# One PSUM rotation of four banks for the attention's scores and for the work beside it

## The chip, the cores and the metric

The kernel runs on one core of a Trainium2 chip. The metric is the device time of one launch in microseconds (us); the median of several runs is compared.

## The reference, cut to what matters

Two layers of a streaming encoder run over 1024 prompt frames and 64 sample frames (T = 1088 columns here). Each layer projects the normalised input once, feeds three token mixers, merges them and adds the result back:

```
h = rmsnorm(x, norm_in)
hq, hkv, g_a, u_b, g_b, qkv_c, g_c, g_mix = split_cols(h @ w_in)
o_a = mla_attend(...) * silu(g_a)          # 8 heads, whole past
o_b = pool_mix(u_b, ...) * silu(g_b)       # trailing means, one linear map a group
o_c = ca_attend(...) * silu(g_c)           # 4 heads, band of chunks, bias
gates = sigmoid(g_mix)
m = gates[0] * (o_a @ w_o_mla) + gates[1] * (o_b @ w_o_pool) + gates[2] * (o_c @ w_o_ca)
x = x + m @ w_out
x = x + sigmoid(rmsnorm(x, ple_norm) @ w_ple_gate) * (ple @ w_ple_proj)
```

## The kernel before, in words

Activations lie feature by token, 128 features to a tile. In each layer a long projection (`gemm`, L404) comes first, then the attention with other work beside it, then the merge of the latent heads' output (`merge`), then the output projection and the `ple` block (again `gemm`). Most products are sums of three matmuls of split operands (`mm3`, L132 to L134).

`attention` runs 108 units a layer, one unit for each head and block of 128 queries: 36 of the four chunk heads, then 72 of the eight latent heads. A unit's `scores` takes one or two tiles `S` of the pool `pg` (L1034 for chunk heads, L1105 for latent ones); DVE takes their minimum (L1036, L1109); ACT makes the exponentials (L857); DVE the reciprocal of the sum (L864) and POOL the product with it (L865). Two units later TensorE transposes the result into `pT` (L891), which ACT and DVE split into `PT`, and multiplies it with the values (`pv`, L925, L917).

Three further pieces of work go beside this. `ple_proj` makes `pps` (32 tiles of 6 matmuls, copied by ACT at L1444 into one of two buffers `o` and stored as `pp`). `pool_branch` makes `pbm` (6 tiles), from which `mbo` is stored. `merge_bc` loads `mbo` and the chunk heads' output through two buffers `of`, splits them into eight tiles `oh`, `ol`, and then does 16 works: a work loads two gates `g` (tags `g8` and `g16`, two buffers each, 272 KB a load), makes four tiles `mps` of 6 matmuls, multiplies them into the gates on DVE (L1424), adds the gates on POOL (L1426) and stores the sum as `mb` from the buffer `g8`. A gate buffer is free for the work after next only when the store from it has landed. `merge` loads `mb` after the attention.

The order on each engine is not written out: the scheduler of the tile framework hoists or delays instructions by priority, and pools hand out their buffers in the order of the program text. In the program text `beside` (which is all of `pps`, `pbm` and `mps`) is called by `attention` ahead of the scores of the 14th unit from the end (`BESIDE = 14`). Only the first steps of the two generators run earlier, through `advance`. DMAs all go through SP's queue in one order; a DMA that waits holds those behind it.

PSUM has eight banks. In the attention, before the change, `pg` has three for `S`, `pn` two for `pT`, `po` one for `pps`, `pbm` and `mps`, and `pv` two.

Of the kernel before, what the change touches and what calls it, by code (L numbers as in the profile page):

```python
# [10 lines left out]
F32 = mybir.dt.float32  # L11
# [35 lines left out]
AT_E = (("K00", KT, 1), ("Q00", T, 1), ("Q10", T, 1), ("K10", KT, 1))  # L47

BANKS = {"gemm": (("pg", 3), ("pn", 2)), "keys": (("pg", 2), ("pn", 2), ("po", 2)),
         "attn": (("pg", 3), ("pn", 2), ("po", 1), ("pv", 2))}  # L50
LATE = 100
NEAR, BESIDE = 8, 14
PVE = ("v",)
# [22 lines left out]
class K:  # L76
# [1223 lines left out]
    def pool_branch(self, l, sp):  # L1300
        nc, d = self.nc, self.d
        zd = self.z_d[l]
        W = 1120
        for j in range(2):
            wr = sp.tile([128, 128], F32, tag="pw", name="pw")
            self.ld(wr, d["poolw"][l, j])
            u = sp.tile([128, W], F32, tag="pu", name="pu")
            nc.gpsimd.memset(u[:, 0:16], 0.0)
            nc.gpsimd.memset(u[:, 1040:1041], 0.0)
            self.ld(u[:, 16:1040], zd[Z_UB + j][:, :1024])  # L1310
            self.ld(u[:, 1041:1056], d["hist"][l, j])
            self.ld(u[:, 1056:], zd[Z_UB + j][:, 1024:])
            self.st(d["poolp"][l, j], u[:, 1025:1040])
            self.st(d["pools"][l, j], u[:, 1105:1120])
            g = self.r
            self.ld(g, zd[Z_GB + j])
            yield
            a = sp.tile([128, W], F32, tag="pa", name="pa")
            b = sp.tile([128, W], F32, tag="pb", name="pb")

            def dbl(dst, src, s, p0=0):
                n = 2
                for i in range(n):
                    c0, c1 = max(s, W // n * i), W // n * (i + 1)
                    nc.gpsimd.tensor_add(dst[p0:, c0:c1], src[p0:, c0:c1], src[p0:, c0 - s:c1 - s])
                nc.scalar.copy(dst[p0:, :s], src[p0:, :s])

            dbl(a, u, 1)
            yield
            if j == 0:  # L1330
                dbl(b, a, 2, 64)
                nc.scalar.copy(b[:64], a[:64])
            else:
                dbl(b, a, 2)
                yield
                dbl(a, b, 4)
                yield
                dbl(b, a, 8, 64)
                nc.scalar.copy(b[:64], a[:64])
            yield  # L1340
            pl = sp.tile([128, T], F32, tag="pl", name="pl")
            sc = self.pinv[:, j, 16:17]
            nc.vector.scalar_tensor_tensor(pl[:, :1024], b[:, 16:1040], sc, u[:, 16:1040], op0=ALU.mult, op1=ALU.subtract)
            nc.vector.scalar_tensor_tensor(pl[:, 1024:], b[:, 1056:], sc, u[:, 1056:], op0=ALU.mult, op1=ALU.subtract)
            nc.vector.tensor_mul(b[:, 16:32], b[:, 16:32], self.pinv[:, j, :16])
            nc.vector.tensor_sub(pl[:, :16], b[:, 16:32], u[:, 16:32])
            yield
            hi = sp.tile([128, T], F32R, tag="pa", name="ph")
            lo = sp.tile([128, T], F32R, tag="pb", name="plo")
            n = 2  # L1350
            for i in range(n):
                c = slice(T // n * i, T // n * (i + 1))
                self.split(pl[:, c], hi[:, c], lo[:, c], "a", 'v')
            wh = sp.tile([128, 2, 128], F32R, tag="pwh", name="pwh")
            self.split(wr, wh[:, 0], wh[:, 1])
            yield
            yield
            o = sp.tile([128, T], F32, tag="pl", name="po")
            for c0, c1 in CH3:
                ps = self.po.tile([128, 512], F32, tag="o", name="pbm")  # L1360
                self.mm3(ps[:, :c1 - c0], wh[:, 0], wh[:, 1], hi[:, c0:c1], lo[:, c0:c1])
                nc.vector.scalar_tensor_tensor(o[:, c0:c1], ps[:, :c1 - c0], self.gn[l][:, G_PS + j:G_PS + j + 1],
                                               g[:, c0:c1], op0=ALU.mult, op1=ALU.mult)
                yield
            self.ld(self.mbo_d[l][j], o)
# [37 lines left out]
    def merge_bc(self, l, sp):  # L1403
        nc, d = self.nc, self.d
        zd = self.z_d[l]

        def weights(m):
            return self.weights(d["wbc"][l, m], 4)

        def gates(m, ti):  # L1410
            gs = []
            for k in (8, 16):
                gs.append(sp.tile([128, H], F32, tag=f"g{k}", name="g"))
                self.ld(gs[-1], zd[Z_MIX + k + m][:, ti * H:ti * H + H])
            return gs

        def work(ti, m, hl, w, gs):
            for g, b in zip(gs, (0, 2)):
                for c in range(2):
                    cc = slice(c * C, c * C + C)  # L1420
                    ps = self.po.tile([128, 512], F32, tag="o", name="mps")
                    for k in (b, b + 1):
                        self.mm3(ps[:, :C], w[:, 0, k], w[:, 1, k], hl[k][0][:, cc], hl[k][1][:, cc], k == b, k == b + 1)
                    nc.vector.tensor_mul(g[:, cc], g[:, cc], ps[:, :C])  # L1424
                yield
            nc.gpsimd.tensor_add(gs[0], gs[0], gs[1])  # L1426
            self.ld(self.mb_d[l][m][:, ti * H:ti * H + H], gs[0])

        yield from self.ahead(sp, [self.mbo_d[l][0], self.mbo_d[l][1], self.o_d[l][0], self.o_d[l][1]], weights, work, gates)

    def ple_proj(self, l, sp, op):
        nc, d = self.nc, self.d

        def weights(m):
            return self.weights(d["wpp"][l, m], 2)

        def work(ti, m, hl, w, _):
            o = op.tile([128, H], F32, tag="po", name="o", bufs=2)
            for c in range(2):
                cc = slice(c * C, c * C + C)  # L1440
                ps = self.po.tile([128, 512], F32, tag="o", name="pps")
                for k in range(2):
                    self.mm3(ps[:, :C], w[:, 0, k], w[:, 1, k], hl[k][0][:, cc], hl[k][1][:, cc], k == 0, k == 1)
                nc.scalar.copy(o[:, cc], ps[:, :C])  # L1444
            yield
            self.ld(self.pp_d[l][m][:, ti * H:ti * H + H], o)

        yield from self.ahead(sp, [d["p"][l, 0], d["p"][l, 1]], weights, work, els=("g", "v"))
# [234 lines left out]
```

## Time and profile before

| what | us |
|---|---|
| median of 3 runs | 2279.34 (2278.78 to 2288.59) |
| the profiled execution: time | 2290.6 |
| the profiled execution: span of the core | 2288.8 |
| PE busy in the span | 2163.4 (95%) |
| PE weight loads busy | 2083.9 (91%) |
| DVE busy | 1743.5 (76%) |
| ACT busy | 1176.3 (51%) |
| POOL busy | 693.4 (30%) |

PE is TensorE's matmuls. The span begins with the first instruction and ends with the last. The attention takes two stretches of it, one for each layer. A table of stretches gives the length, then the busy time of each engine with its count of instructions, then the granted clock of TensorE as a share of 2.4 GHz, the DMA engines' busy share, and GB/s.

### The profile page before, as it was taken

The numbers are of one execution on the slowest core, as the hardware profiler recorded it, in microseconds if no ns is written. First come the engines' busy times: TensorE is split into PE (matmuls) and PEld (weight loads), VectorE is DVE, ScalarE is ACT, GpSimd is POOL, SyncE is SP. The second block draws the span as 40 slices with busy tenths as digits, with TensorE's granted clock in tenths as the row PEclk, the third lists the DMA queues.
The fourth block names the chain that finished last, engine by engine and source line by source line (L and its number), as shares of the span: only waits on it lengthen the run. The fifth ranks groups of instructions, "written<-read, shape, count | busy, mean of one in ns | idle before, by whom it ended". The sixth has DMA issues, their size and how long they took to land.

```text
span 2288.8 us, 44876 instructions
## 1 busy us (share of the span) xinstructions
PE 2163.4 (95%) x16326; PEld 2083.9 (91%) x16326; DVE 1743.5 (76%) x3590; ACT 1176.3 (51%) x2491; POOL 693.4 (30%) x918
## 2 busy tenths in 40 slices
PE   5999999999789999899989999999988899999998
PEld 4999999999588998899979999999987889998998
DVE  8777888676568889887686678876747788889764
ACT  6234455454667666335453343555546776653341
POOL 0000044676455554000000000547574665430000
PEclk8999999999899999999989999999999999999999
DMA  3534546455966764545634345554569666645472
GB/s 125 185 110 135 185 142 193 129 158 143 279 196 183 198 172 136 204 173 179 210 107 139 118 158 173 165 157 127 159 179 276 199 186 179 186 162 186 144 232 74
DMA packets 222191, 385.81 MB, mean 169 GB/s; under 512 B 30404, under 2 KB 114196, under 8 KB 221972
## 3 DMA queue, kind: packets, MB, share of 16 engines
q1 hardware_dynamic: 221972, 382.95, 54.2%
q8 instruction: 130, 2.13, 0.4%
q14 instruction: 89, 0.73, 0.1%
HBM read 248.16 MB, written 134.70 MB: 167 GB/s over the span
## 4 chain that ended last, share of the span: by engine, by line
PE 62%; DMA 15%; DVE 13%; ACT 4%; issue 3%; POOL 2%; SPq 1%; DVEq 0%; ACTq 0%; POOLq 0%
PE g L404 36%; PE g L372 6%; PE S L1105 3%; PE pv L925 3%; PE pT L891 3%; DMA pp<-o 3%; DMA g<-z 2%; PE mps L132 1%; DMA mb<-g 1%; SPq L87 1%; DVE wop L121 1%; DMA r<-rd 1%; PE mps L134 1%; PE mps L133 1%; PE vps L1074 1%
## 5 line engine op out<-in xcount | busy, mean ns | idle before, releaser
L110 ACT CAST wop<-wraw 128x512 fp32r<-128x512 f32 (+1 forms) x238 | 143.8, 606 | 259.3 <-PE g L404 154.8
L865 POOL TENSOR_SCALAR P<-P,st 128x640 f32<-128x640 f32 (+8 forms) x216 | 155.3, 723 | 203.0 <-DVE st L864 122.3
L121 POOL TENSOR_TENSOR wop<-wraw,wop 128x512 fp32r<-128x512 f32 (+1 forms) x80 | 99.3, 1244 | 382.9 <-ACT wop L110 382.4
L121 DVE TENSOR_TENSOR PT<-pT,PT 128x512 fp32r<-128x512 f32 (+4 forms) x360 | 167.6, 473 | 39.3 <-ACT PT L110 37.3
L121 DVE TENSOR_TENSOR wop<-S,wop 128x512 fp32r<-128x512 f32 x178 | 141.6, 795 | 68.1 <-ACT wop L110 67.6
L110 ACT CAST wop<-S 128x512 fp32r<-128x512 f32 x202 | 124.6, 618 | 123.4 <-PE g L404 119.6
L110 ACT CAST PT<-pT 128x512 fp32r<-128x512 f32 (+4 forms) x360 | 147.0, 420 | 54.4 <-PE pT L891 47.8
L404 PE MATMUL g<-B11h,wop 128*128 128x272 f32 x832 | 152.4, 294 | 16.5 <-ACT B11h L112 12.7
L925 PE MATMUL pv<-PT,V 128*128 128x256 f32 x928 | 165.4, 297 | 2.5 <-DVE PT L121 1.6
L1105 PE MATMUL S<-K,Q 96*128 96x384 f32 (+5 forms) x672 | 158.8, 353 | 6.5 <-ACT P L857 6.5
L132 PE MATMUL mps<-oh,wop 128*128 128x272 f32 x512 | 155.2, 304 | 8.6 <-DVE g L1424 3.9
L891 PE MATMUL pT<-ident,P 128*128 128x128 f32 x936 | 158.5, 279 | 2.9 <-DVE PT L121 1.2
L404 PE MATMUL g<-T3h,wop 128*128 128x272 f32 x832 | 153.9, 293 | 7.7 <-ACT T3h L110 5.0
L404 PE MATMUL g<-B21h,wop 128*128 128x272 f32 x832 | 156.3, 298 | 4.8 <-ACT P L416 4.6
L404 PE MATMUL g<-T1h,wop 128*128 128x272 f32 x832 | 151.7, 293 | 3.6 <-DVE z L681 1.9
L404 PE MATMUL g<-T2h,wop 128*128 128x272 f32 x832 | 152.9, 294 | 2.1 <-ACT T2h L110 1.8
L404 PE MATMUL g<-B22h,wop 128*128 128x272 f32 x832 | 151.0, 293 | 0.0
L404 PE MATMUL g<-T4h,wop 128*128 128x272 f32 x832 | 149.7, 291 | 0.0
L134 PE MATMUL mps<-oh,wop 128*128 128x272 f32 x512 | 148.3, 290 | 0.0
L857 ACT ACTIVATE P<-S,st 128x384 f32<-128x384 f32 (+5 forms) x224 | 126.7, 572 | 38.2 <-DVE st L853 27.1
L925 PEld LDWEIGHTS pv<-PT,V 128*128 128x128 f32 x928 | 131.1, 191 | 11.0 <-DVE PT L121 6.2
L404 PEld LDWEIGHTS g<-B11h,wop 128*128 128x128 f32 x832 | 124.0, 192 | 18.1 <-ACT B11h L112 13.2
(291 smaller groups left out, 6591.0 us busy)
## 6 DMA issues: line engine op xcount, KB each, us to landing
wraw<-win SPq DMA_DIRECT2D x88, 512.0 KB
z<-z SPq DMA_DIRECT2D x96, 272.0 KB
g<-z SPq DMA_DIRECT2D x64, 272.0 KB
z<-z SPq DMA_DIRECT2D x24, 544.0 KB
Q<-q SPq DMA_DIRECT2D x32, 408.0 KB
K<-k SPq DMA_DIRECT2D x32, 400.0 KB
k<-hl SPq DMA_DIRECT2D x48, 256.0 KB
q<-hl SPq DMA_DIRECT2D x64, 192.0 KB
```

What stands on the lines that cost most here:

```text
L87: self.nc.sync.dma_start(out=self.raw(out), in_=self.raw(in_))
L110: nc.scalar.copy(out, src)
L121: e.tensor_sub(out, src, hi)
L132: mm(ps, lhsT=wh, rhs=xh, start=first, stop=False)
L134: mm(ps, lhsT=wl, rhs=xh, start=False, stop=last)
L372: self.nc.tensor.matmul(ps[:, c, :C], lhsT=hl[kh][:, w, kb, :], rhs=b[:, kb, c * C:(c + 1) * C], start=kh + k == 0, stop=kh == 1 and k == 11)
L404: nc.tensor.matmul(ps[:, c, :C], lhsT=hl[:, w, kb, :], rhs=b[:, kb, c * C:(c + 1) * C], start=k == 0 and not more, stop=k == 11, skip_grou ...
L857: nc.scalar.activation(u.p[:, c * w:c * w + w], x, AF.Exp, bias=st[:, 0:1], scale=-1.0, accum_out=st[:, 2 + c:3 + c])
L865: nc.gpsimd.tensor_scalar(u.p[:, :n], u.p[:, :n], st[:, 4:5], 1.0, op0=ALU.mult, op1=ALU.mult)
L891: nc.tensor.transpose(ps[:, j], p[:, c0:c0 + 128], self.ident)
L925: nc.tensor.matmul(ps[:, :w], lhsT=v(b), rhs=grp[b // 4][:, b % 4, j, :w], start=i + j == 0, stop=i == len(bl) - 1 and j == 1)
L1105: nc.tensor.matmul(ps[:, :ww], lhsT=q[0:96, q0:q0 + 128], rhs=k[0:96, k0 + c * w:k0 + c * w + ww], start=i == 0, stop=i == 2 and not diag)
```

## The change

The pool `po` goes, its bank is given to `pg`, and `pps`, `pbm` and `mps` are taken from `pg` under the tag `s` of the scores. No instruction is added or removed.

```
 BANKS = {"gemm": (("pg", 3), ("pn", 2)), "keys": (("pg", 2), ("pn", 2), ("po", 2)),
-         "attn": (("pg", 3), ("pn", 2), ("po", 1), ("pv", 2))}
+         "attn": (("pg", 4), ("pn", 2), ("pv", 2))}
...
             for c0, c1 in CH3:
-                ps = self.po.tile([128, 512], F32, tag="o", name="pbm")
+                ps = self.pg.tile([128, 512], F32, tag="s", name="pbm")
...
                     cc = slice(c * C, c * C + C)
-                    ps = self.po.tile([128, 512], F32, tag="o", name="mps")
+                    ps = self.pg.tile([128, 512], F32, tag="s", name="mps")
...
                 cc = slice(c * C, c * C + C)
-                ps = self.po.tile([128, 512], F32, tag="o", name="pps")
+                ps = self.pg.tile([128, 512], F32, tag="s", name="pps")
```

The change moves instructions. On PE, inside the third latent head of the first layer, this stood before (`S` are scores, `mps` the merge's matmuls):

```order
L925 MATMUL pv<-PT,V 128x256
L891 MATMUL pT<-ident,P 128x128 x4
L1105 MATMUL S<-K_8383,Q_8381 128x384
L1105 MATMUL S<-K_8384,Q_8381 128x384
L1105 MATMUL S<-K_8383,Q_8382 128x384
L925 MATMUL pv<-PT,V 128x256 x7
L891 MATMUL pT<-ident,P 128x128 x4
L925 MATMUL pv<-PT,V 128x256
L132 MATMUL mps<-oh,wop 128x272
L133 MATMUL mps<-ol,wop 128x272
L134 MATMUL mps<-oh,wop 128x272
```

and this stands there now:

```order
L925 MATMUL pv<-PT,V 128x256
L1105 MATMUL S<-K_8380,Q_8378 128x384
L1105 MATMUL S<-K_8381,Q_8378 128x384
L1105 MATMUL S<-K_8380,Q_8379 128x384
L925 MATMUL pv<-PT,V 128x256 x7
L891 MATMUL pT<-ident,P 128x128 x7
L1105 MATMUL S<-K_8380,Q_8378 128x384
L1105 MATMUL S<-K_8381,Q_8378 128x384
L1105 MATMUL S<-K_8380,Q_8379 128x384
```

No `pps`, `pbm` or `mps` is left among the first 94 units of a layer. All of them stand behind the scores of the 94th unit: first `pps` with the transposes and values of the last units in flight, then the rest of `pps`, `pbm`, and 384 `mps` matmuls in one block. On PE, the end of that block and the scores of the 95th unit behind it (before, `mps` stood between such scores):

```order
L134 MATMUL mps<-oh,wop 128x272
L132 MATMUL mps<-oh,wop 128x272
L133 MATMUL mps<-ol,wop 128x272
L134 MATMUL mps<-oh,wop 128x272
L1105 MATMUL S<-K_9706,Q_9704 128x288
L1105 MATMUL S<-K_9707,Q_9704 128x288
L1105 MATMUL S<-K_9706,Q_9705 128x288
```

On SP, in the same layer, the stores of `mb` and the loads of gates stood before between the loads of the next head (`Q`, `K`):

```order
L87 DMA mb_109<-g 128x544
L87 DMA g<-z_105 128x544 x2
L90 DMA o_111<-o 128x1088
L87 DMA acc<-z_105 128x1088
L87 DMA wraw<-woa 128x4x128
L87 DMA mb_109<-g 128x544
L87 DMA g<-z_105 128x544 x2
L87 DMA Q_9707<-q_117 96x1088
L87 DMA Q_9708<-q_117 96x1088
```

and now they follow each other, with the loads of all heads ahead of them:

```order
L87 DMA mb_109<-g 128x544
L87 DMA g<-z_105 128x544 x2
L87 DMA wraw<-woa 128x4x128
L87 DMA mb_109<-g 128x544
L87 DMA g<-z_105 128x544 x2
L87 DMA mb_109<-g 128x544
```

What moved is the place of the beside work: it was spread over the attention, and is now one block ahead of the last 14 units.

## Rows read from the trace of the kernel before

**Rows 1.** Table of stretches: chunk and latent part of layer 0, then of layer 1.

```profile
core 0: us, PE busy (x) PEld busy (x) DVE busy (x) ACT busy (x) POOL busy (x), PEclk, DMA share, GB/s
590.90:692.60 101.70, 85.65 (x577) 76.78 (x577) 71.70 (x262) 68.53 (x201) 50.12 (x82) 0.95 0.84 228
692.60:910.00 217.40, 210.55 (x1584) 193.09 (x1583) 184.18 (x529) 146.06 (x427) 115.59 (x164) 1.00 0.60 171
...
1724.60:1823.00 98.40, 84.44 (x578) 75.71 (x578) 71.81 (x262) 68.53 (x201) 50.36 (x82) 0.97 0.86 236
1823.00:2040.00 217.00, 210.96 (x1584) 193.07 (x1583) 184.82 (x529) 146.54 (x427) 115.57 (x164) 1.00 0.60 172
```

**Rows 2.** Timeline: reciprocals of units 1, 10, 37 and 108 (start us, us, engine, line).

```profile
590.87 0.17 DVE L864 RECIPROCAL st<-st 128x1 f32<-128x1 f32 x1 [1.03 <-ACT P L857]
...
606.04 0.17 DVE L864 RECIPROCAL st<-st 128x1 f32<-128x1 f32 x1 [0.19 <-ACT P L857]
...
692.58 0.15 DVE L864 RECIPROCAL st<-st 128x1 f32<-128x1 f32 x1
...
904.29 0.17 DVE L864 RECIPROCAL st<-st 128x1 f32<-128x1 f32 x1
```

**Rows 3.** Timeline: matmuls of `pps` back to back, at full clock, then at half.

```profile
576.48 0.29 PE L133 MATMUL pps<-ol,wop 128*128 128x272 f32 x1
...
576.61 0.29 PE L134 MATMUL pps<-oh,wop 128*128 128x272 f32 x1
...
576.73 0.29 PE L132 MATMUL pps<-oh,wop 128*128 128x272 f32 x1
...
590.25 0.43 PE L133 MATMUL pps<-ol,wop 128*128 128x272 f32 x1
...
590.47 0.43 PE L134 MATMUL pps<-oh,wop 128*128 128x272 f32 x1
...
590.70 0.43 PE L132 MATMUL pps<-oh,wop 128*128 128x272 f32 x1
```

**Rows 4.** Groups of instructions, 692.6 to 910 us: DVE, POOL and ACT beside the latent heads.

```profile
L1424 DVE TENSOR_TENSOR g<-g,mps 128x272 f32<-128x272 f32 x64 | 27.4, 428 | 4.5 <-DMA g<-z 3.8 <-PE mps L134 0.3
...
L1426 POOL TENSOR_TENSOR g<-g 128x544 f32<-128x544 f32 x16 | 22.1, 1379 | 15.4 <-DVE st L864 6.4 <-DVE st L863 5.8 <-DVE g L1424 2.4
...
L121 POOL TENSOR_TENSOR ol<-of,oh 128x544 fp32r<-128x544 f32 x8 | 10.7, 1350 | 1.4 <-ACT oh L110 1.4
...
L110 ACT CAST oh<-of 128x544 fp32r<-128x544 f32 x8 | 5.0, 658 | 3.4 <-DMA of<-o 2.4 <-DMA of<-mbo 1.0
```

**Rows 5.** Groups on ACT, 572 to 692.6 us: the copies of `pps`.

```profile
L1444 ACT COPY o<-pps 128x272 f32<-128x272 f32 x32 | 12.3, 385 | 21.0 <-DMA pp<-o 13.8 <-PE pps L134 6.0 <-ACT P L857 0.8
```

**Rows 6.** SP's own waits, 690 to 965 us (total, times, longest).

```profile
SPq L87 <- DMA mb<-g: 48.7, 15, 8.2
```

**Rows 7.** Chain of waits: a store and a load of 272 KB; later the merge's first gate.

```profile
744.82 9.60 DMA mb<-g
754.43 2.66 DMA g<-z
...
913.49 6.89 DMA g<-z
```

**Rows 8.** Timeline of SP: store of `mbo`; the second of two loads waits for it.

```profile
697.05 0.34 SPq L87 DMA_DIRECT2D mbo<-po  x1
697.44 2.93 SPq L87 DMA_DIRECT2D of<-mbo  x2
```

**Rows 9.** Table of stretches in which PE waited often (columns of Rows 1).

```profile
575.00:590.00 15.00, 7.94 (x32) 6.59 (x33) 7.17 (x17) 7.64 (x15) 8.70 (x11) 0.70 1.01 305
620.00:635.00 15.00, 10.21 (x57) 9.36 (x55) 7.81 (x29) 6.65 (x19) 5.68 (x10) 0.77 1.04 240
```

**Rows 10.** Instructions on the tile `mb`: its 16 stores in the first layer.

```profile
L87 SPq DMA_DIRECT2D mb<-g x16: 319/328/611, 724.4 to 912.3; - x16
```

## The prediction

> **What bounds the kernel now.** I read the table of stretches first. In the latent part of a layer PE is busy for 210.55 of 217.40 us and DVE for 184.18; in the chunk part PE has 85.65 of 101.70, and the DMA engines are 0.84 busy [rows 1]. The second layer reads alike, so I work out one layer and double it. The reader is to see that the latent part is a stretch that PE fills, and fills partly with work that is no attention: the `mps` matmuls. The chunk part is not full on any engine; its first head, which had little beside it, took from 590.87 to 606.04, 15.2 us, while all four took 101.7 (to 692.58) [rows 2]. The latent heads took 211.7 more, to 904.29 [rows 2]. These 313.4 us a layer are what the change touches. The merge's stores of `mb` end at 912.3, with the attention itself, so before, the beside work just fits [rows 10].
>
> Next I read what a work beside costs by itself. Matmuls of 272 columns start 0.125 to 0.13 us apart at full clock, and 0.22 to 0.23 apart at half [rows 3]; I use 0.126 and 0.226. So the 24 matmuls of an `mps` work are 3.0 us of PE, and 12 of a `pps` work 1.5 us. But a work also has a loop around its buffers: load of a gate, four products of 0.428, one sum of 1.379, a store, and only then the next load into that buffer [rows 4, 6]. SP waited 15 times for a landing `mb` store, 48.7 us in all, 3.25 each [rows 6]. As long as the loop lies beside attention, nobody pays for it.
>
> **The change part by part.** No instruction is added. The pools hand out buffers in the order of the text, and now the scores of the last 14 units stand behind `beside` in the same pool. The order of instructions shows the outcome: no beside matmul among the first 94 units, and then all of it in one block before the 95th unit's scores. The fourth bank is worth little to the scores in this order, and the sum has these terms.
>
> 1. *Chunk heads without filler.* Bounds: 60.7 us (four times the first head's 15.2) and 101.7 (nothing gained). I take 68, 17 a head, near the low end: the `pp` stores leave SP's queue and the DMA engines in this stretch. Gain 33.7.
>
> 2. *Latent heads without filler.* PE loses 384 x 0.126 = 48.4 us, so at an unchanged packing 211.7 becomes 163.3. DVE would then have 184.18 - 27.4 = 156.8 to do in the same time [rows 1, 4], so two engines would be 96% full at once, which a chain from PE to DVE, ACT, POOL and back does not reach. I take 7% on it, 175. Bounds 163.3 and 211.7. Gain 36.7.
>
> 3. *The block: `pps`.* Each of 16 works needs one of two `o` buffers: two copies of 0.385 [rows 5], an issue of 0.33, and a landing. For the landing there are two near rows: a store that took 9.60 us [rows 7], and the mean wait of 3.25 plus an issue between, some 3.65 [rows 6]. I take 3.65, because the long one shared the engines with the loads of a head, and in the block no head is loaded. That is 4.75 us for two works, 2.4 each, 38 us (PE alone: 24). `pbm` adds 2.
>
> 4. *The block: its middle.* The store of the second `mbo` takes 3.0 us until the load behind it is issued (697.44 + 2.93 - 0.32 - 697.05) [rows 8]. Then a tile needs a load of 2.66 [rows 7], a cast of 0.66 and a subtraction of 1.35 [rows 4]: 7.7 us to the first `mps` matmul with nothing for PE. Eight tiles go through two buffers, so three more rounds of 5.0 follow, and the first two works end about 25 us after `pbm`. Before, attention covered this; now nothing does.
>
> 5. *The block: `mps`.* The loop is 2.66 + 4 x 0.428 + 1.38 + 3.65 and three issues, 1.0: 10.4 us for two works, 5.2 each. PE needs 3.0 of it, DVE 1.7, POOL 1.4, so the loop decides. The other 14 works take 73 us. Bounds: 3.0 a work (PE alone) and 12.5, the pace of before ((912.3 - 724.4) / 15) [rows 10]; I am nearer to the lower, since that pace was set by attention between the works.
>
> The block is 38 + 2 + 25 + 73 = 138 us.
>
> 6. *Filling again.* DVE, ACT and POOL run dry of attention in the block, and the 95th unit starts from its scores: about one unit, 211.7 / 72 = 3 us.
>
> 7. *The merge's head.* `mb` is now stored long before the attention ends, so the first gate's 6.89 us at 913.49 can be hidden behind the last units [rows 7]. Gain 7; bounds 0 and 7.
>
> A layer: -33.7 - 36.7 + 138 + 3 - 7 = +63.6; two layers +127. The profiled execution took 2290.6 and would take 2418. The median of the runs is 11.3 lower, 2279.34, so I predict **2406**.
>
> What a load or store should cost without company is also stated by the Trainium skill (DMA: Bandwidth & Descriptors, Anatomy of one DMA): about 2.0 us fixed and 436 GB/s, fitted on another issue path, which gives 2.64 us for 272 KB. The load of 2.66 agrees, the store of 9.60 does not [rows 7]. With 2.64 for the stores as well, by that page, an `mps` work would take 4.7 and a `pps` work 1.9 us, and the kernel 2376.
>
> **The rivals.**
>
> *Stores stay slow (0.10).* If a store takes 9.60 us in the block too [rows 7], an `mps` work takes (10.4 + 5.95) / 2 = 8.2 us and a `pps` work 5.35: 42 + 47 = 89 us more a layer, 2584. Against it: SP's list has no head loads there any more.
>
> *Half clock (0.15).* PE is busy half of the time in the block. Where it was busy for 7.94 of 15 us the mean granted clock was 0.70 of 2.4 GHz, and 0.77 for 10.21 of 15 [rows 9]; part of these stretches ran at 1.2 GHz. If the whole block does, 12 slower matmuls lengthen the loop by 1.2 to 11.6 us and a `pps` work takes 12 x 0.226 = 2.7: 8 + 5 us a layer, 2432. The Trainium skill (TensorE: Matmul & The Clock Gate, Part 1) says that the throttled state is the default and that activity releases it. These two stretches agree.
>
> *Attention gains nothing in the latent part (0.12).* If the chain through one unit sets 211.7, and not PE's fill, term 2 goes: +36.7 a layer, 2480. Against it is PE at 97% there [rows 1].
>
> *The block runs at PE's pace (0.05; the other side).* PE runs ahead by a work through four banks. If loads and stores overlap so well that matmuls alone count, `mps` takes 14 x 3.0 = 42 and `pps` 24 (31 and 14 less), and if the attention also reaches 60.7 and 163.3 (19 less), a layer changes by 63.6 - 64 = 0: 2279, no change. It decides from a block of 74 us on, with the attention as forecast. Two buffers and the wait of 3.25 us speak against it [rows 6].
>
> That the work isn't moved at all is excluded by the order.
>
> **How the numbers follow.** The forecast has 0.56; 0.02 is left for what I don't see. The range: with attention at its floors (19 less a layer) and stores of 2.66 (15 less) it is 2338, and a little more overlap of `pps` with the last units gives 2320; with no gain in the latent part and a chunk part of 80 it is 2504. So 2320 to 2505, which holds the half clock and the latent rival and leaves out slow stores and PE's pace. A measurement of this kernel can tell about 0.5%, 11 us, from no change. Slower 0.94; the same 0.04, nearly all from the last rival; faster 0.02, if the block is denser still.
>
> **What would show it.** In the changed profile two stretches a layer should stand out: latent heads at about 22 us each in place of 26.5, with PE below 97%, and a block of some 140 us with PE half busy, DVE under 40%, and no `P` or `pT` work behind its first 10 us. SP should wait for `mb` stores there, and the `mps` works should lie 5 us apart. I am wrong if the block is shorter than 110 us, if `mps` works lie 3 us apart, if latent heads keep 26 us, or if clock and not the loop paces the block.

## The result and the profile after

The changed kernel takes **2436.07 us** (median of 4 runs, 2433.19 to 2436.89). The kernel before took 2282.4 on the same chip (2278.78 to 2288.59). The ratio is 1.0661, with a 95% interval of 1.0643 to 1.0678: slower by 154 us. Forecast were 2406 and a ratio of 2406 / 2279.34 = 1.0556.

The page of the changed kernel begins like this; behind it stands the row of the engines from the page of the kernel before:

```profile
span 2433.6 us, 44898 instructions
...
PE 2220.9 (91%) x16326; PEld 2112.0 (87%) x16326; DVE 1735.2 (71%) x3590; ACT 1175.0 (48%) x2491; POOL 693.0 (28%) x918
```

```profile
PE 2163.4 (95%) x16326; PEld 2083.9 (91%) x16326; DVE 1743.5 (76%) x3590; ACT 1176.3 (51%) x2491; POOL 693.4 (30%) x918
```

Every engine has the same count of work; the page's whole count, 44898 against 44876, differs by 22 instructions that no engine counts as work. PE runs the same 16326 matmuls and is busy 57.5 us longer than before, with a granted clock of 0.957 in the mean (before: 0.976). This is a first hint of stretches at half clock.

The table of stretches, columns as in [rows 1]. The first four rows are layer 0: chunk heads, latent units 37 to 94, the gap between units 94 and 95, the last 13 intervals. Then come three pieces of the gap (`pps` to the first product of `mps`, its filling, the other `mps` works), then chunk, latent, gap and last intervals of layer 1:

```profile
588.68:669.71 81.03, 69.46 (x400) 55.89 (x399) 61.86 (x250) 54.45 (x157) 33.79 (x66) 0.90 0.81 205
669.71:815.90 146.19, 133.62 (x957) 117.83 (x958) 120.45 (x366) 105.34 (x331) 62.86 (x109) 0.99 0.44 110
815.90:949.10 133.20, 100.25 (x648) 92.45 (x647) 42.88 (x96) 31.75 (x78) 57.75 (x48) 0.86 0.64 205
949.10:977.80 28.70, 24.98 (x161) 20.79 (x160) 25.21 (x71) 21.94 (x66) 11.79 (x20) 0.94 0.43 160
812.60:863.70 51.10, 38.42 (x270) 36.83 (x270) 15.86 (x30) 24.26 (x66) 21.02 (x21) 0.88 0.59 198
863.70:888.40 24.70, 19.14 (x94) 16.77 (x95) 4.99 (x12) 5.14 (x8) 14.47 (x11) 0.63 0.47 151
888.40:946.40 58.00, 44.59 (x301) 40.98 (x300) 22.81 (x56) 4.33 (x7) 22.68 (x18) 0.94 0.72 225
...
1792.80:1871.30 78.50, 67.31 (x400) 53.35 (x399) 61.51 (x250) 54.53 (x157) 33.77 (x66) 0.93 0.81 211
1871.30:2017.50 146.20, 133.62 (x958) 117.91 (x959) 120.38 (x367) 105.59 (x331) 62.85 (x109) 0.99 0.44 110
2017.50:2149.30 131.80, 99.37 (x650) 91.79 (x648) 43.25 (x97) 32.49 (x80) 57.26 (x48) 0.87 0.66 209
2149.30:2179.90 30.60, 26.37 (x159) 21.28 (x157) 25.18 (x71) 21.46 (x62) 11.78 (x20) 0.91 0.39 144
```

The first stretch answers to the 101.7 us and the three behind it to the 211.7 us that the prediction took from [rows 1, 2]. The attention of layer 0 now takes 81.0 + 146.2 + 133.2 + 28.7 = 389.1 us against 313.4: +75.7. In layer 1 it takes 387.1 us against 309.8 (first to last reciprocal, 1724.56 to 2034.35 before): +77.3. The two make 153 us. Outside of the attention some 8 us less were spent, so that the span is 145 longer. The medians differ by 154 and not by 145, because the profiled execution before, at 2290.6 us, lies 8 us above its median.

So the change did what the order said. The heads became faster without filler, by 20.7 us in the chunk part and some 36.8 in the latent part. One block without attention, 133 us in each layer, takes back more than twice that.

How the block spends its time shows in the chain of waits. Here are three stores of `pps` outputs, then one round of the `mps` loop:

```profile
820.26 6.43 DMA pp<-o
...
837.80 5.25 DMA pp<-o
...
849.57 3.91 DMA pp<-o
...
904.03 1.38 POOL g L1426
905.43 2.88 DMA mb<-g
908.32 3.17 DMA g<-z
...
911.61 0.80 DVE g L1424 x2
...
912.53 1.37 POOL g L1426
```

The reader is to see a loop on transfers: sum, store of `mb`, load of the next gate, products, next sum, 8.5 us for two works. PE is not in this round. A work ahead of it shows the other case. Its 24 matmuls start 0.23 us apart, the spacing at half clock [rows 3], and stand on the chain themselves, from 893.25 to 899.02:

```profile
893.25 0.59 PE mps L132
...
898.83 0.19 PE mps L134
```

That is 5.8 us where 24 matmuls need 3.0 at full clock [rows 3]. In the whole chain from 886 to 950 us the two transfers have 48% and the `mps` matmuls 12%. SP's own waits, 864 to 950 us, and the times of the second and the last sums (the first row holds the second and the third) say the same:

```profile
SPq L87 <- DMA mb<-g: 21.5, 15, 2.7
```

```profile
887.12 2.64 POOL L1426 TENSOR_TENSOR g<-g 128x544 f32<-128x544 f32 x2
...
946.42 1.34 POOL L1426 TENSOR_TENSOR g<-g 128x544 f32<-128x544 f32 x1 [2.23 <-DVE g L1424]
```

From the second sum to the last, 14 works take 59.3 us: 4.24 each. SP waited 15 times for a landing store of `mb`, as before [rows 6], but 1.43 us each in place of 3.25.

### The profile page after: what moved, and what is told of

The parts are those of the page before. It is cut to its first block, busy times and chain, and to the rows that moved or that the text cites. A ratio compares the mean times of both kernels' runs of the same rounds, so it can differ in the third digit from the quotient of the medians.

```text
span 2433.6 us, 44898 instructions
## 1 busy us (share of the span) xinstructions
PE 2220.9 (91%) x16326; PEld 2112.0 (87%) x16326; DVE 1735.2 (71%) x3590; ACT 1175.0 (48%) x2491; POOL 693.0 (28%) x918
## 4 chain that ended last, share of the span: by engine, by line
PE 60%; DVE 14%; DMA 11%; ACT 5%; issue 4%; POOL 4%; SPq 1%; DVEq 0%; ACTq 0%; POOLq 0%
PE g L404 33%; PE g L372 5%; PE pv L925 4%; PE S L1105 3%; PE pT L891 2%; PE mps L133 2%; PE mps L134 2%; PE mps L132 2%; DMA mb<-g 2%; DVE PT L121 1%; DMA g<-z 1%; ACT P L857 1%; DMA pp<-o 1%; DVE st L1109 1%; DVE wop L121 1%
## 5 line engine op out<-in xcount | busy, mean ns | idle before, releaser
L925 PE MATMUL pv<-PT,V 128*128 128x256 f32 x928 | 179.1, 310 | 19.8 <-DVE PT L121 10.1
L132 PE MATMUL mps<-oh,wop 128*128 128x272 f32 x512 | 157.1, 312 | 41.8 <-DVE g L1424 26.0
L121 DVE TENSOR_TENSOR PT<-pT,PT 128x512 fp32r<-128x512 f32 (+4 forms) x360 | 168.2, 474 | 31.7 <-ACT PT L110 27.0
L1105 PE MATMUL S<-K,Q 96*128 96x384 f32 (+5 forms) x672 | 168.3, 367 | 20.2 <-ACT P L857 18.9
L925 PEld LDWEIGHTS pv<-PT,V 128*128 128x128 f32 x928 | 136.6, 199 | 39.0 <-DVE PT L121 21.2
L134 PE MATMUL mps<-oh,wop 128*128 128x272 f32 x512 | 154.6, 303 | 0.0
L132 PEld LDWEIGHTS mps<-oh,wop 128*128 128x128 f32 x512 | 102.7, 203 | 50.6 <-DVE g L1424 22.0
```

Of the source, the lines that this page charges most:

```text
L121: e.tensor_sub(out, src, hi)
L132: mm(ps, lhsT=wh, rhs=xh, start=first, stop=False)
L134: mm(ps, lhsT=wl, rhs=xh, start=False, stop=last)
L925: nc.tensor.matmul(ps[:, :w], lhsT=v(b), rhs=grp[b // 4][:, b % 4, j, :w], start=i + j == 0, stop=i == len(bl) - 1 and j == 1)
L1105: nc.tensor.matmul(ps[:, :ww], lhsT=q[0:96, q0:q0 + 128], rhs=k[0:96, k0 + c * w:k0 + c * w + ww], start=i == 0, stop=i == 2 and not diag)
```

## The experiments

**The theory** is that of the prediction, with its parts: the place of the beside work in the one order of banks makes the block; the block is paced by transfers through two buffers, and not by PE. **The rivals**: one rotation for two sorts of work costs by itself, wherever it stands; or PE and its clock pace the block. All ratios below are to the kernel before on the same chip.

### 1. One rotation, but handed out step by step

```
-            near.setdefault(BESIDE, []).append(lambda: self.beside(l))
+            first, second = self.beside_steps(l)
+            for i in range(100):
+                for _ in range((i % 2 == 0) if i < 40 else (i - 39) * 42 // 60 - (i - 40) * 42 // 60):
+                    near.setdefault(108 - i, []).append(lambda s=first if i < 40 else second: next(s, None))
+            near.setdefault(68, []).insert(0, lambda: list(first))
+            near.setdefault(9, []).append(lambda: list(second))
...
```

`first` is the text of `pps` and `pbm`, `second` that of `merge_bc`; the new method that hands them out one step at a time (`beside_steps`) is left out of the edit above. The banks stay those of the change.

> The changed kernel with its one rotation of four, but the text of the program hands out the banks of the beside work step by step between the units (pps and pbm between the first 40 units, mps between the next 60) instead of all at once ahead of the last 14 units. Theory A (what costs is the place of the block in the one order of banks, not the sharing): the block of 131 to 133 us between the 94th and 95th unit is gone, the attention of a layer is back at 305 to 320 us, and the kernel takes 2265 to 2300 us. Rival B (one rotation for two sorts of work costs by itself, since a score must wait for the bank of a beside work that waits for a load): chunk heads and latent heads both become longer than before, the attention of a layer takes 340 us or more, and the kernel 2350 us or more.

Measured: 2306.51 us, ratio 1.0113 (1.0096 to 1.0131). Its stretches in layer 0 (chunk; latent without beside work; latent with `mps`; the last units):

```profile
590.66:691.13 100.47, 88.97 (x578) 77.00 (x576) 71.31 (x261) 69.27 (x199) 49.54 (x80) 0.95 0.84 235
691.13:733.60 42.47, 35.12 (x208) 29.49 (x209) 29.04 (x85) 27.53 (x82) 23.69 (x33) 0.88 0.62 176
733.60:898.18 164.58, 160.95 (x1227) 150.25 (x1227) 136.48 (x388) 102.04 (x297) 82.46 (x113) 1.00 0.63 181
898.18:918.51 20.33, 17.24 (x120) 14.33 (x119) 18.10 (x51) 15.95 (x46) 9.15 (x15) 1.00 0.46 174
```

There is no block, and where `mps` lies beside attention PE is 98% busy. The place is worth 5.5 of the 6.6%, some 125 us. The time is 6 us above the upper end that theory A gave and 44 below what B asked for: A holds for the bulk, and 26 us (1.1%) remain to be explained.

### 2. The same, with the `mps` steps begun earlier

```
-                for _ in range((i % 2 == 0) if i < 40 else (i - 39) * 42 // 60 - (i - 40) * 42 // 60):
-                    near.setdefault(108 - i, []).append(lambda s=first if i < 40 else second: next(s, None))
-            near.setdefault(68, []).insert(0, lambda: list(first))
+                for _ in range(i % 2 == 0 if i < 36 else 1 if i < 46 else (i - 45) * 32 // 54 - (i - 46) * 32 // 54):
+                    near.setdefault(108 - i, []).append(lambda s=first if i < 36 else second: next(s, None))
+            near.setdefault(72, []).insert(0, lambda: list(first))
```

> The step by step version with its one rotation of four (2306.5 us), but the mps steps begin at the 37th unit in place of the 41st and are spread to the 100th, so that few latent units are without them. Theory A (that version lost its 27 us against the kernel before because 42 us of a layer ran without any beside work and PE was full only behind that; sharing itself costs nothing): the attention of a layer falls from 327 to 311 to 320 us and the kernel takes 2272 to 2295 us. Rival B (a score that stands behind a beside work in the one rotation costs this time): it stays at 2300 to 2312 us.

Measured: 2317.28, ratio 1.015 (1.0124 to 1.0175). Theory A's gain did not come. The median lies above B's range too, but the interval touches that of experiment 1. PE's own waits from 690 to 760 us, and the chain there, show one cost of this text:

```profile
PE mps L132 <- ACT oh L110: 4.4, 1, 4.4
```

```profile
717.44 8.95 DMA of<-mbo
726.42 0.65 ACT oh L110
727.11 0.82 PE mps L132 x2
...
731.74 0.68 PE S L1110 x3
```

The text now placed an `mps` matmul where its tile had not landed, a load of 8.95 us beside attention. PE ran nothing for 4.4 us, and the next scores on the chain come behind this matmul, at 731.74. In one rotation, the text has to guess when a load will be there. That such waits make up the whole difference is not shown.

### 3. The step by step text, with the banks of before

The text of experiment 1, with the diff of the change undone (`pg` 3 and `po` 1, and `po` for the three sorts of work).

> The banks of the kernel before (three for scores, one of its own for the beside work), with the step by step text of the first version that spread the work. Theory A (where the beside work has its own bank, the place in the text does not decide when it runs): the beside work keeps about the places it has in the kernel before, and the time stays within 10 us of 2280. Rival B (the step by step text costs 27 us by itself, whatever the banks): about 2306 us.

Measured: 2283.99, ratio 1.001 (0.9995 to 1.0024). The text alone costs nothing. With a bank of their own, the beside works keep about their places under this text too: the stores of `mb` in layer 0 begin between 720.8 and 914.1 us, and between 724.4 and 912.3 before [rows 10]. Experiments 1 and 3 differ by the banks alone, so the shared rotation costs those 1% at this placement.

### 4. The step by step text, with four buffers a gate

```
-                gs.append(sp.tile([128, H], F32, tag=f"g{k}", name="g"))
+                gs.append(sp.tile([128, H], F32, tag=f"g{k}", name="g", bufs=4))
```

> The first step by step version (one rotation of four, 2306.5 us) with four buffers for each gate. Theory C (what the shared rotation still costs there is a score behind an mps work that waits for its loaded gate): 2283 to 2296 us. Rival D (it is what lies ahead of the first mps work, the of tiles and the units without beside work, which gates do not touch): within 6 us of 2306.

Measured: 2308.99, ratio 1.0097 (1.0066 to 1.0127). Rival D holds: gates are not what the shared rotation waits for there. Whether a better placement by hand gets those 26 us back is open; the one other that I tried was worse.

### 5. The change with four buffers a gate

The edit of experiment 4 in the changed kernel; the order of instructions is that of the change.

> The changed kernel with four buffers for each of the two gates of the mps works in place of two. Theory A (the loop of load, four products, sum and store through two buffers paces the block): the 14 later mps works lie 3.0 to 3.4 us apart in place of 4.24, the block is 10 to 17 us shorter in each layer, and the kernel takes 2400 to 2416 us. Rival B (PE and its clock pace these works): they stay 4.0 to 4.3 us apart and the kernel stays within 5 us of 2436.

Measured: 2401.92, ratio 1.0535 (1.0516 to 1.0555), 34 us less than the change by the medians and 29 by the ratios. The second and the last sums of layer 0 (the first row holds three sums):

```profile
884.80 3.99 POOL L1426 TENSOR_TENSOR g<-g 128x544 f32<-128x544 f32 x3
...
927.68 1.35 POOL L1426 TENSOR_TENSOR g<-g 128x544 f32<-128x544 f32 x1 [1.40 <-DVE g L1424]
```

The stretch between them:

```profile
886.00:928.00 42.00, 39.88 (x302) 39.37 (x300) 24.62 (x54) 4.34 (x7) 23.02 (x19) 0.96 0.87 284
```

14 works in 42.9 us, 3.06 each in place of 4.24: PE's 24 x 0.126 = 3.0 [rows 3], and PE is busy for 39.88 of 42 us. So two buffers paced the works, and only with four does PE. Theory A is shown.

### 6. The change with a third of the `mps` matmuls

```
-                        self.mm3(ps[:, :C], w[:, 0, k], w[:, 1, k], hl[k][0][:, cc], hl[k][1][:, cc], k == b, k == b + 1)
+                        nc.tensor.matmul(ps[:, :C], lhsT=w[:, 0, k], rhs=hl[k][0][:, cc], start=k == b, stop=k == b + 1)
```

> The changed kernel with the mps matmuls cut to the high by high product: the two products with a low part are left out, 8 matmuls a work in place of 24. Theory A (the buffer loop paces the mps works of the block): they stay 3.8 to 4.3 us apart. Rival B (PE paces them): they come 2 us closer, to about 2.2 us, and the block is 28 us shorter in each layer, 2380 us for the kernel. If both share it, a value between.

Measured: 2423.56 (one run). The second and the last sums, and the stretch between them:

```profile
882.70 1.34 POOL L1426 TENSOR_TENSOR g<-g 128x544 f32<-128x544 f32 x1
...
940.50 1.34 POOL L1426 TENSOR_TENSOR g<-g 128x544 f32<-128x544 f32 x1 [1.93 <-DVE g L1424]
```

```profile
885.00:941.00 56.00, 33.09 (x107) 25.18 (x107) 23.19 (x57) 3.79 (x7) 23.16 (x19) 0.52 0.73 232
```

4.13 us a work. Two thirds of the `mps` matmuls gone, and the clock at 0.52, nearly all of the stretch at 1.2 GHz: the pace changed by 0.1 us. The block became 5.6 us shorter (127.6), not the 28 that B asked for. So PE does not pace these works in the change. Of its clock this run tells less, since it also took away the matmuls that a low clock makes longer; the one work at half clock shown above cost 2.8 us of 59.3.

### 7. The change with four buffers for the outputs of `pps`

```
-            o = op.tile([128, H], F32, tag="po", name="o", bufs=2)
+            o = op.tile([128, H], F32, tag="po", name="o", bufs=4)
```

> The changed kernel with four buffers for the output tiles o of the pps works in place of two. Theory A (term 3: two buffers and their stores pace pps in the block): the copies of pps in the block, 813 to 851 us before, spread over 24 to 30 us in place of 38; 8 to 14 us less a layer, 2408 to 2420 us for the kernel. Rival B (PE paces them, with the last attention work beside it): 36 to 39 us as before, and the kernel within 6 us of 2436.

Measured: 2430.83, ratio 1.0626 (1.0599 to 1.0652), 5 to 8 us less than the change, with intervals that touch. The copies of `pps` in layer 0, in the change and then here:

```profile
L1444 ACT COPY o<-pps x32: 376/387/424, 813.7 to 853.8; 128x272 f32<-128x272 f32 x32
```

```profile
L1444 ACT COPY o<-pps x32: 385/387/423, 813.1 to 844.8; 128x272 f32<-128x272 f32 x32
```

What ACT waited for ahead of these copies, in the change and then here:

```profile
  DMA pp<-o: 11.7, 5
```

```profile
  PE pps L134: 7.5, 15
```

40.1 us became 31.7, between the two theories, while the kernel's time lies within the 6 us of 2436 that rival B gave. With two buffers the copies waited for stores, with four for PE. The buffers held `pps` up, but the sums of `mps` come only some 7 us sooner (the second at 880.34), and the gap of layer 0 shrinks by 3 us, to 130.0. Term 3 had the right loop and overrated how much hangs on it.

### 8. Both kinds of buffers

> The changed kernel with four buffers both for the gates of the mps works and for the output tiles of pps. If the two loops are separate pieces of the block, as terms 3 and 5 have it, the gains add: 34 us of the gates (measured) and that of the output tiles, by theory A of the run before this one 2374 to 2386 us. Rival B (they share the queue and the DMA engines, so that one gain takes the other's place): 2395 to 2405 us. What is left of the block then, about 110 us a layer, is PE's own time and the filling in its middle.

Measured: 2392.5, ratio 1.0471 (1.0434 to 1.0507). By the ratio it is 15 us under experiment 5, between A and B. The gap of layer 0 goes from 133.2 to 113.2 us (120.7 in experiment 5, 130.0 in experiment 7), 20.0 us where the single gains make 15.7. So the gains add, and rival B fails, though the median is nearer to its range than to A's. With both loops widened the kernel is still 4.7% slower than before: a block without attention costs with four buffers too.

### 9. Gates with four buffers in the kernel before

The edit of experiment 4 in the kernel before.

> The kernel before with four buffers for each gate, the control to the same edit in the changed kernel. Theory A (before, the buffer loop lies beside attention and nobody waits for it): within 10 us of 2280. Rival B (PE's fill in the latent part hangs on the gates): under 2268 us.

Measured: 2295.13 beside 2286.07, ratio 1.0042 (1.0027 to 1.0057). The median lies beyond the 10 us around 2280 that theory A gave; but this chip's kernel before lies 6 us above 2280 itself, and against it the edit costs 0.4%. The edit that gave the change some 30 us gives the kernel before nothing. As the prediction had it, nobody pays for the loop while it lies beside attention.

### 10. Only `mps` in the scores' rotation

```
-                    ps = self.po.tile([128, 512], F32, tag="o", name="mps")
+                    ps = self.pg.tile([128, 512], F32, tag="s", name="mps")
```

In the kernel before, with its three banks.

> The kernel before with only the mps works moved to the rotation of the scores (three banks); pps and pbm keep the bank po. Theory A (each sort of beside work that joins the scores' rotation becomes a block at its place in the text): the chunk heads take about 102 us as before, the latent units 2.5 to 2.6 us each in place of 2.94, and the block holds mps alone: about 29 us for its filling and 59 for 14 works. The attention of a layer takes 40 to 55 us more than before, and the kernel 2360 to 2395 us. Rival B (the fourth bank that the scores share matters, or the stores' company): outside of that, near 2282 or near 2436.

Measured: 2391.98, ratio 1.0489 (1.047 to 1.0509). Chunk, latent units 37 to 94, and gap of layer 0:

```profile
587.08:686.50 99.42, 85.22 (x578) 76.14 (x577) 71.83 (x261) 68.39 (x201) 50.11 (x82) 0.96 0.85 232
686.50:842.50 156.00, 138.38 (x958) 117.08 (x957) 124.41 (x369) 110.58 (x335) 72.67 (x116) 1.00 0.49 131
842.50:920.40 77.90, 62.40 (x444) 57.87 (x443) 35.61 (x83) 10.69 (x23) 30.30 (x24) 0.97 0.63 204
```

The sort that joins the rotation becomes a block, the others stay: theory A, with sizes off. The gap is 77.9 and not 88, since the `of` tiles ahead of `mps` were now loaded and split beside the latent heads (691 to 727 us); the latent units take 156.0 / 57 = 2.74 us and not 2.5 to 2.6. With `mps` alone in the rotation, some 110 of the 154 us are there.

This stretch gives another number. The change has the same units with the same 957 or 958 matmuls and no filler in 146.19 us, but with four banks for the scores. So a fourth bank is worth at most about 10 us of 156 where no `mps` stands between: the splitting of the `of` tiles lies in this stretch too (POOL has 72.67 us here and 62.86 in the change), and no run separates the two. The prediction took the fourth bank as worth little.

### 11 and 12. Another bank for the scores, another bank for the beside work

Both in the kernel before, both paid with one of the two `pv` banks: `pg` 4, `po` 1, `pv` 1, and `pg` 3, `po` 2, `pv` 1.

> The kernel before with a fourth bank for the scores, taken from the outputs of the heads (pg 4, pv 1); the beside work keeps its own bank. What a fourth bank is worth to the scores, less what one pv bank costs. Theory A (the scores gain little from a fourth bank, as the prediction took it): 2275 to 2310 us. Rival B (the fourth bank lets the scores run ahead and fills PE): under 2270 us.

> The kernel before with a second bank for the beside work, taken from the outputs of the heads: po 2 and pv 1 in place of po 1 and pv 2. Theory A (with two banks of their own the beside works run earlier and closer together, and attention pays for it with one pv bank): mps is done 40 us earlier, latent units with mps become longer, those without shorter; PE has the same work, so the kernel is within 25 us of 2280, rather above it. Rival B (PE fills better with a second bank): 2255 to 2270 us.

Measured: 2348.35, ratio 1.0296 (1.0276 to 1.0316), and 2379.19, ratio 1.0437 (1.0409 to 1.0465). Both slower, and outside of what any theory of mine gave. In both the latent part has a stretch of some 20 us in which the attention slows down: DVE is busy for 9.41 of 19.50 us in one (from 755.3) and for 8.02 of 20.30 in the other (from 758.1). The chain through the first, in the version with four score banks:

```profile
750.99 8.35 DMA mb<-g
...
759.36 3.36 DMA g<-z
...
762.84 0.45 DVE g L1424
...
763.33 0.59 PE mps L132
```

With another set of banks the order on PE changed too, and an `mps` work stands there whose gate is not loaded. The runs don't tell apart what one `pv` bank costs and what this order costs, so what a fourth bank gives to scores with beside work between them stays open.

No run beat the kernel before; experiment 3 equals it.

## Why the prediction was right, and where its sizes were off

The direction, the mechanism and the range held: 2436 lies in 2320 to 2505, a wide range. The terms came out less well than the sum, since their misses partly cancel. None of the four conditions for "wrong" came true. The forecast for the attention of a layer was +70.6 us (terms 1 to 6), and +75.7 and +77.3 came; the merge was to give back 7, and gave 0.4 in layer 0.

- **Term 1, chunk heads: missed.** 68 us were forecast, 17 a head; 81.0 and 78.5 came, so 13 and 10.5 us of gain failed. Heads 1, 2 and 4 of layer 0:

```profile
588.68:607.58 18.90, 14.82 (x73) 11.52 (x73) 13.25 (x55) 11.64 (x32) 7.80 (x14) 0.74 1.04 302
607.58:627.49 19.91, 17.28 (x108) 13.62 (x109) 15.77 (x67) 13.97 (x41) 9.35 (x18) 1.00 1.01 233
...
648.11:669.71 21.60, 19.80 (x119) 16.09 (x117) 17.09 (x65) 14.89 (x46) 7.40 (x16) 0.92 0.52 120
```

The step that failed was to take the first head's 15.2 us [rows 2] as the pace of all four. Transposes and weighing lag some units behind the scores, so a first head has 73 records of matmuls and the later ones 107 to 119, which keep PE busy for 17 to 20 us. PE's busy time alone, 69.46 us, is more than the 68 that I gave to the whole part. The reason for the low end failed too: without the `pp` stores the DMA engines are as busy in the first two heads as before (1.04 and 1.01; 1.02 and 1.04 before). Besides, without `pps` beside it, PE was granted 0.74 in the first head: part of it ran at 1.2 GHz, and it took 18.9. In experiment 10, where `pps` stayed, a first head took 15.18 us at 0.97. That the filler had kept the clock up fits these two heads. The Trainium skill (TensorE: Matmul & The Clock Gate, Part 1) says that activity releases the throttle; these two heads agree. No run changed the filler alone, and in experiment 3 a first head with 103 records, filler among them, took 21.48 us at 0.82; so how much of the 18.9 us the clock cost stays open.

- **Term 2, latent heads: right.** 146.2 + 28.7 = 174.9 us in layer 0 and 176.8 in layer 1; 175 were forecast. PE was busy for 133.62 of 146.19 us there, 91%. That the size fits to 0.1 us is in part luck: the 7% was a guess, and with three banks the same units took up to 10 us longer (experiment 10).

- **Terms 3 to 5, the block: 138 forecast, 130.5 came** (133.2 without the refill of 2.7 us between the last sum and unit 95). `pps`: 38.3 from unit 94 to the last copy's end at 854.23 (38). This agreement is luck: term 3 lets every pair of works wait for a store of 3.65 us, but the copies waited five times, 11.7 us in all, for stores of up to 6.43 us. `pbm`: 3.1 (2). Filling: 29.8 from there to the second sum (25). Fourteen `mps` works: 59.3 (73). The last is the largest miss. The loop was the right one, as experiments 5 and 6 show, but of its four products only two lie on the chain (the `x2` row above). The chain has 1.38 + 2.88 + 3.17 + 0.80 and small issues, 8.5 us for two works, where I added 10.4. The stores also landed sooner than the 3.65. That was no landing time but SP's mean wait and an issue, and a wait begins only when SP comes to it: in the block a store took 2.88 us where SP waited 1.43 in the mean.

- **The page's time for a transfer.** By the Trainium skill (DMA: Bandwidth & Descriptors, Anatomy of one DMA) 272 KB take an estimated 2.64 us. Store and load of the round shown took 2.88 and 3.17, so the page was closer here than my 3.65. Beside attention a store took 9.60 [rows 7]. The page would have given 4.7 us a work, with all four products; 4.24 came.

- **Term 6, refill:** 2.7 against 3, right.

- **Term 7, the merge's head: missed.** I gave 7 us for the hidden gate. In layer 0 the merge's first product with a gate comes 15.4 us after the last reciprocal, in place of 17.4, but its last `mps` matmul 56.7 us after it, in place of 57.1. What is late next is the last weighing, behind which the first merge matmul stands:

```profile
982.63 2.72 PE pv L925 x11
985.35 0.23 PE mps L132
```

From there the merge starts at half clock (0.23 us). Its stretch was granted 0.94, and the 57.1 us from 910 before 1.00. PE is busy for 55.17 of 56.70 us, so the half clock lies on the merge's path and takes back part of the hidden gate:

```profile
977.80:1034.50 56.70, 55.17 (x411) 53.96 (x412) 47.80 (x80) 20.14 (x36) 2.17 (x4) 0.94 0.36 117
```

The misses add up to 13 - 8 + 7 = 12 us a layer; 63.6 were forecast and 75.3 came in layer 0, merge included. Some 9 us of the two layers' sum came back outside of attention and merge: 2.2 ahead of layer 0's attention (its first reciprocal comes at 588.68 in place of 590.87), 4.8 between the two layers' merge and attention, 2 behind. In the 18 to 19 us ahead of each attention the kernel before had run some 28 `pps` matmuls, which are now in the block. That they left is a likely reason for the first two of these gains, and the prediction's sum had no term for it. Of "what would show it" two things were wrong. Transposes `pT` still ran 15 us into the block (to 831), not 10. And PE is busy for 100 of the block's 133 us, not half, in part since its granted clock of 0.86 made the matmuls longer.

Of the rivals, *stores stay slow* and *PE's pace* are excluded by 4.24 us a work, *no gain in the latent part* by 146.2 us for 57 units. *Half clock* is there, 0.63 while the block fills, but paces little: of the 14 works one, by 2.8 us, and 14 `pps` matmuls that stand 0.23 apart on the chain (844.5 to 847.6), by some 1.4.

## What to carry over

Buffers of one rotation are handed out in the order of the text, so two sorts of work that share one are tied to that order. Work that was spread by its inputs' readiness turns into a block at its place in the text. Before sharing a bank, ask not how often the bank is idle but what freedom of order its owner has from it: here one bank was worth 154 us with the text as it stood, and still 24 to 26 with the text rewritten to spread the work. And a loop through two buffers that is free beside other work becomes the bound once it stands alone; price it then by its chain, counting only what lies on it.

## What I had not expected of the hardware

The same 272 KB store took 9.60 us beside attention [rows 7] and 2.88 in the block, where SP waited 1.43 us for such stores in the mean and not 3.25. The mean granted clock fell from 0.976 to 0.957, so by its two levels TensorE spent an estimated 8.6% of the span at 1.2 GHz in place of 4.8%, some 99 us more. Yet cutting the `mps` matmuls to a third, in a stretch at 0.52, moved the pace of the works from 4.24 to only 4.13 us.
